# The MLP's u and gate products of two token pieces in seven products of halves for eight (Strassen's algorithm), with values and gated result kept in DRAM

## The chip, the cores and the metric

The kernel runs on one core of a Trainium2 chip. The core has five engines, each with its own queue that it works off in order: TensorE (PE: matrix products; PEld is its weight load), VectorE (DVE), ScalarE (ACT), GpSimd (POOL) and SyncE (SP), which here issues all DMAs. Products land in PSUM, a small memory that the other engines empty into SBUF; DRAM lies outside. The metric is device time in microseconds (us) of one execution. The kernel before has a median of 961.26 us in 3 runs (960.9 to 961.68).

## The reference

One inference step of two layers on 1024 prompt tokens and 64 sample tokens (8 sequences of 8), width 1024. The first layer is a gated linear attention, which the change leaves alone. The second is the one at stake:

```python
def cmlp_mixer(h, w_in, ln_g, ln_b, w_spatial, b_spatial, w_out):
    u, v, gate = jnp.split(h @ w_in, 3, axis=-1)
    v = layernorm(v, ln_g, ln_b)
    ...
    vg = v.reshape(bsz, n, c, CMLP_GROUPS, CMLP_GROUP_DIM)
    mixed = jnp.einsum('gts,bnsgd->bntgd', ws, vg) + bs.T[:, :, None]
    z = u * mixed.reshape(bsz, t, CMLP_WIDTH) * jax.nn.silu(gate)
    return z @ w_out, v
```

Before it, h = rmsnorm(x); behind it, x + z @ w_out goes through a last rmsnorm. The normalised v rows of the sample tokens are an output too.

## The kernel before, in words

The 1088 tokens are cut into three pieces (`PIECES`): piece 0 and piece 1 of 384 tokens (3 chunks of 128), and piece 2 of 256 prompt tokens and the 64 sample tokens. Activations lie transposed, features on the 128 partitions; width 1024 is `KT` = 8 slices of 128. To reach float32 accuracy, every operand of a large product is split into a high and a low part, and a product of slices takes three matmuls: high by high, high by low, low by high.

Weights come in blocks of 256 columns, each in four tiles of 128x512 (two slices by 256 columns). `fetch_w` (L89-97) loads such a tile from DRAM into one of three raw buffers (L93), makes the high part on ACT (L95) and the low part on DVE (L96), into a ring of eight `w` tiles. `fm_block` (L104-112) makes 128 columns of a block for one piece: 24 matmuls (L110) of 384 or 320 columns. `tm_block` and `tm_sample` (L114-142) do it with the tokens as rows. `split` (L167-174) makes the two parts of an activation.

In order of time:
- to about 478 us: the attention layer. To 541: its output product, `out_proj(12, ...)`, which leaves x in `x1_spill` in DRAM and the normed `h1` in SBUF, as parts.
- 541 to 640, the v stage: blocks 16 to 19, 9 groups each. ACT empties each group into the nine tiles of v (`vt`, `vs`) that stay in SBUF, L858; DVE gathers statistics, L864. Behind it the tiles are normalised in place, by ACT (L895) and DVE (L897) in turn.
- 640 to 848, the u/gate stage, L907-943: m = 0 to 7, one block (20 + m) each, with 128 columns of u and 128 of gate. For each piece: the gate product; DVE's scaling by the tokens' norm `rs` (L919); Silu on ACT (L920); a second scaling on POOL (L921); the mixing matmuls of v with `ws` (L924); gain and bias on DVE (L926); the u product; two DVE products (L935, L936) that leave z in SBUF. `fetch_w` gets the next block. `v_out` (L899-905) writes the sample rows of v. In m=7 z is split into `zs`.
- 848 to the end: `out_proj(28, ...)` on `zs`, and the last norm (L945-951).

A list scheduler in the build orders each engine's instructions from the program, by estimated times; so matmuls of different products stand interleaved, and the order on each engine is fixed before the launch. A tile with one buffer can be loaded again only when its last reader is done. SP too works in order: a DMA that waits holds all behind it.

Of the kernel before, what the change touches and what calls it, by code (L numbers as in the profile page):

```python
# [38 lines left out]
def trunk_kernel(ctx: ExitStack, tc: tile.TileContext, a: dict):  # L39
# [852 lines left out]
    for i, t in enumerate(tiles):  # L892
        r = t.shape[0]
        if i % 2:
            A.activation(t, t, AF.Identity, bias=lt[:r, i:i + 1], scale=lr[:r, i:i + 1])  # L895
        else:
            V.tensor_scalar(t, t, mv[:r, i, 0:1], lr[:r, i:i + 1], ALU.subtract, ALU.mult)  # L897

    def v_out(m):  # L899
# [3 lines left out]
        G.tensor_tensor(bc[:, 2, :], vs[:, cs], bc[:, 0, :], ALU.mult)  # L903
# [3 lines left out]
    z = [rp.tile([P, KT, n], F32, tag=f"raw{p}", name=f"z{p}") for p, n in enumerate(size)]  # L907
    zs = [None] * 3
    for m in range(KT):
        w = ws_[20 + m]  # L910
        g = m // 2
        fs = slice(m * P, (m + 1) * P)
        bias = mp.tile([P, P], F32, tag="bias", bufs=2, name="bias")
        V.scalar_tensor_tensor(bias, rsum[:, g, :], lnb[:, m:m + 1], bs[:, g, :], ALU.mult, ALU.add)
        for p, (t0, n, nch) in enumerate(PIECES):
            np_ = nch * P
# [2 lines left out]
            V.tensor_tensor(sg, ga, rs[p], ALU.mult)  # L919
            A.activation(sg, sg, AF.Silu)  # L920
            G.tensor_tensor(sg, sg, rs[p], ALU.mult)  # L921
# [149 lines left out]
```

## Time and profile before

| what | value |
|---|---|
| median of 3 runs | 961.26 us (960.9 to 961.68) |
| the profiled execution | 961.62 us, of which 959.8 us are the span that the profile shows |
| mean granted PE clock in it | 0.991 |
| DMA over the span | 77.62 MB, mean 81 GB/s |
| output product and norm, 848 to 960 us: PE busy | 100.58 of 112 us |

The page shows, under its second heading, the busy share of 40 equal slices in tenths. The u/gate stage is slices 27 to 35 (24 us each):

```profile
PE   8989999999999999989999999999999999999995
DVE  7888777677785787677543932254333333562246
ACT  8664545453553555363343622232111111353322
POOL 2023331323233232222241300004111011101123
```

A row of a group names line, engine and operation, what it writes and reads, its shape, its count, then busy time in us and mean ns of one, then the engine's idle time before them and what ended it. A chain row has start, length and what ran.

### The profile page before, as it was taken

What the parts mean: (1) busy time and instruction counts of PE and PEld (TensorE: products, weight loads), DVE (VectorE), ACT (ScalarE), POOL (GpSimd) and SP (SyncE); (2) the same over time, 40 slices, a digit from 0 to 9 for tenths busy, and PEclk for the clock granted to TensorE, in tenths of its full rate; (3) what the DMA queues carried; (4) which work ended last, traced back from release to release, by engine and by line L of the source; (5) the groups of instructions that cost most, each with busy time, mean ns of one, the idle gap of its engine ahead of it and who ended that gap; (6) DMA issues with size and microseconds to landing.
All of it is one profiled execution on the core that took longest, in us unless ns stands there. A gap on an engine that the chain in (4) does not pass through costs nothing.

```text
span 959.8 us, 16108 instructions
## 1 busy us (share of the span) xinstructions
PE 928.8 (97%) x6245; PEld 902.2 (94%) x6245; DVE 562.2 (59%) x1188; ACT 386.5 (40%) x800; POOL 210.4 (22%) x236
## 2 busy tenths in 40 slices
PE   8989999999999999989999999999999999999995
PEld 7979989999999899978999999999999999999994
DVE  7888777677785787677543932254333333562246
ACT  8664545453553555363343622232111111353322
POOL 2023331323233232222241300004111011101123
PEclk9999999999999999979999999999999999999998
DMA  9302113310231112423574321112101111123233
GB/s 294 91 1 81 51 34 88 106 44 29 78 114 36 61 62 72 130 90 105 159 248 153 93 70 45 45 45 83 31 26 44 44 45 44 45 59 92 60 112 128
DMA packets 71161, 77.62 MB, mean 81 GB/s; under 512 B 8470, under 2 KB 67676, under 8 KB 71084
## 3 DMA queue, kind: packets, MB, share of 16 engines
q1 hardware_dynamic: 71084, 76.58, 25.7%
q8 instruction: 49, 0.80, 0.3%
q14 instruction: 28, 0.23, 0.1%
HBM read 59.05 MB, written 17.51 MB: 80 GB/s over the span
## 4 chain that ended last, share of the span: by engine, by line
PE 73%; DVE 12%; ACT 5%; issue 4%; DMA 3%; POOL 1%; SPq 0%; DVEq 0%; ACTq 0%; POOLq 0%
PE fm L110 45%; PE tm L124 16%; PE sc L486 2%; PE mix L924 2%; DMA wr<-w 2%; PE o L591 1%; PE pst L552 1%; PE o L560 1%; PE tms L140 1%; PE o L562 1%; DVE scT L499 1%; DVE xl L451 1%; DVE w L96 1%; DVE xl L448 1%; ACT w L95 1%
## 5 line engine op out<-in xcount | busy, mean ns | idle before, releaser
L110 PE MATMUL fm<-h,w 128*128 128x384 f32 (+1 forms) x2208 | 388.9, 332 | 0.1
L110 PEld LDWEIGHTS fm<-h,w 128*128 128x128 f32 x2208 | 365.3, 188 | 2.2 <-DVE h L174 0.7
L124 PE MATMUL tm<-w,h 128*128 128x256 f32 (+1 forms) x1536 | 192.5, 282 | 0.3 <-DVE w L96 0.2
L124 PEld LDWEIGHTS tm<-w,h 128*128 128x128 f32 x1536 | 185.1, 188 | 1.6 <-DVE w L96 0.5
L96 DVE TENSOR_TENSOR w<-wr,w 128x512 fp32r<-128x512 f32 (+1 forms) x128 | 90.9, 726 | 34.5 <-ACT w L95 34.1
L110 PE MATMUL fm<-og,w 128*128 128x384 f32 (+1 forms) x576 | 104.1, 337 | 0.3 <-ACT og L170 0.3
L95 ACT ACTIVATE w<-wr 128x512 fp32r<-128x512 f32 (+1 forms) x128 | 78.3, 626 | 60.4 <-DMA wr<-w 36.6
L110 PEld LDWEIGHTS fm<-og,w 128*128 128x128 f32 x576 | 97.4, 192 | 2.1 <-DVE og L171 0.5
L110 PE MATMUL fm<-zs,w 128*128 128x384 f32 (+1 forms) x576 | 97.2, 330 | 0.4 <-DVE x L793 0.4
L110 PEld LDWEIGHTS fm<-zs,w 128*128 128x128 f32 x576 | 95.9, 188 | 1.3 <-DVE x L793 0.7
L920 ACT ACTIVATE sg<-sg 128x384 f32<-128x384 f32 (+1 forms) x24 | 12.2, 507 | 128.6 <-DVE sg L919 128.6
L793 DVE TENSOR_TENSOR x<-fm,res 128x384 f32<-128x384 f32 (+1 forms) x40 | 21.1, 528 | 69.5 <-PE fm L110 69.5
L921 POOL TENSOR_TENSOR sg<-sg,rs 128x384 f32<-128x384 f32 (+1 forms) x24 | 23.4, 975 | 165.8 <-ACT sg L920 165.8
L772 POOL TENSOR_TENSOR acc<-acc,sq 128x384 f32<-128x384 f32 (+1 forms) x30 | 31.3, 1045 | 110.4 <-ACT sq L767 109.8
L767 ACT ACTIVATE sq<-x 128x384 f32<-128x384 f32 (+1 forms) x42 | 20.9, 503 | 66.8 <-DVE x L793 65.3
L935 DVE TENSOR_TENSOR zt<-fm,zt 128x384 f32<-128x384 f32 (+1 forms) x24 | 12.8, 533 | 54.7 <-PE fm L110 54.7
L864 DVE BATCH_NORM_STATS2 st<-vt 128x6 f32<-128x256 f32 x32 | 13.6, 425 | 52.7 <-ACT vt L858 52.7
L441 POOL TENSOR_TENSOR xe<-xe,k 128x384 f32<-128x384 f32 (+2 forms) x24 | 29.1, 1214 | 45.4 <-ACT xe L440 45.3
L919 DVE TENSOR_TENSOR sg<-fm,rs 128x384 f32<-128x384 f32 (+1 forms) x24 | 12.8, 535 | 42.5 <-PE fm L110 42.5
L858 ACT ACTIVATE vt<-tm 128x256 f32<-128x256 f32 x32 | 12.3, 384 | 61.6 <-PE tm L124 61.6
L622 POOL TENSOR_TENSOR on<-on,g 128x384 f32<-128x384 f32 (+1 forms) x24 | 23.5, 1001 | 58.7 <-DVE on L621 35.9
L448 DVE TENSOR_TENSOR xl<-cum 128x192 f32<-128x192 f32 (+4 forms) x72 | 33.3, 492 | 0.0
(220 smaller groups left out, 1235.7 us busy)
## 6 DMA issues: line engine op xcount, KB each, us to landing
wr<-w SPq DMA_DIRECT2D x124, 256.0 KB, 3.3
s<-s SPq DMA_DIRECT2D x16, 256.0 KB, 5.6
state_s<-ns SPq DMA_DIRECT2D x32, 128.0 KB, 1.7
res<-x_spill SPq DMA_DIRECT2D x16, 192.0 KB, 2.4
y<-x SPq DMA_DIRECT2D x8, 384.0 KB, 2.4
x<-xt SPq DMA_DIRECT2D x7, 384.0 KB, 6.1
og_spill<-on SPq DMA_DIRECT2D x12, 192.0 KB, 1.9
ogr<-og_spill SPq DMA_DIRECT2D x12, 192.0 KB, 2.4
```

The source lines that it names most:

```text
L95: A.activation(w[:, 0], raw, AF.Copy)
L96: V.tensor_tensor(w[:, 1], raw, w[:, 0].bitcast(F32), ALU.subtract)
L110: PE.matmul(acc, lhs, rhs, start=(k == 0), stop=(k == 23))
L124: PE.matmul(acc, lhs, rhs, start=(k == 0), stop=(k == 23))
L441: G.tensor_tensor(xe, xe, kt_[:, :nl], ALU.mult)
L448: V.tensor_tensor(l3[:, :, lo:hi], c3[:, :, (i + 1) * m:], r, ALU.subtract)
L486: PE.matmul(bank[:, c, 0:192], xe[:, c * P:(c + 1) * P], xl[:, c * 192:(c + 1) * 192], start=True, stop=True)
L622: G.tensor_tensor(o, o, gate[h][:, j, t0:t0 + n], ALU.mult)
L767: A.activation(sq, raw[p][:, m, :], AF.Square)
L772: (V if gain is not None and p == 2 or m == KT - 1 else G).tensor_tensor(total, acc[p], sq, ALU.add)
L793: V.tensor_tensor(raw[p][:, m, :], pa, r, ALU.add)
L921: G.tensor_tensor(sg, sg, rs[p], ALU.mult)
```

## The change

For pieces 0 and 1 the block's product is one of 2 by 2 quarters. The rows of the result are u and gate, its columns piece 0 and piece 1; the summed index is cut into even and odd slices. So the weights have four quarters (quarter 1,1: u, even; 1,2: u, odd; 2,1: gate, even; 2,2: gate, odd) and `h1` has four (b11, b21: piece 0 even, odd; b12, b22: piece 1). Eight products of quarters become seven, with four sums of weight quarters (`s1` to `s4`) and four of token quarters (`tsum0` to `tsum3`). A product of quarters is 12 matmuls (`product`, L927). Piece 2 keeps its 48 matmuls of 320 columns.

What goes with it:
- The token sums are made once, in the v stage, one slice pair per block, from `x1_spill` (two DMAs of 384 KB, two ACT scalings, four POOL subtractions, four splits).
- The weight sums are made per block on POOL (L904: four of 128x512), each split on ACT (L891) and DVE (L892), and the plain quarters too: eight `w` tiles per block in place of four. The raw quarters of a block lie in one buffer, `rawq`, loaded by four DMAs of 256 KB (L886).
- v leaves SBUF: each group goes to DRAM (`v1_spill`, L943), and per m its 128 columns come back into one buffer `vm` (L985, L986) and are normalised by nine ACT instructions (L992).
- z goes to DRAM (`z_spill`, L1066 and L1097), and comes back for the split: piece 0 in m=7, pieces 1 and 2 behind the loop.
- The results of the seven products are combined by ACT copies (L1039, L1041, L1046), DVE adds out of PSUM (L1043, L1051, L1053) and POOL adds (L1047, L1048). Two PSUM banks (`two`: pb, pe) and one of the ring (`p1`) are added to by later products, behind the readers of the earlier ones.

```diff
-    vt = [mp.tile([P, D], F32, tag=f"vt{i}", name=f"vt{i}") for i in range(8)]
...
+    def raw_quarters(blk):
+        rw = mp.tile([P, 4, 2, 256], F32, tag="rawq", name="rawq")
+        for i in range(4):
+            SP.dma_start(rw[:, i], a["w256"][blk, i])
+        return rw
+
+    def parts_of(src):
+        w = wp.tile([P, 2, 4, P], F32R, tag="w", bufs=8, name="wq")
+        A.activation(w[:, 0], src, AF.Copy)
+        V.tensor_tensor(w[:, 1], src, w[:, 0].bitcast(F32), ALU.subtract)
+        return w
...
+        def sum(self, x, y, op):
+            t = wp.tile([P, 4, P], F32, tag="raw", bufs=3, name="qsum")
+            G.tensor_tensor(t, x, y, op)
+            return t
+
+        def sums(self):
+            q = self.q
+            s1 = self.sum(q[2, 1], q[2, 2], ALU.add)
+            s2 = self.sum(s1, q[1, 1], ALU.subtract)
+            self.w["s2"] = parts_of(s2)
+            self.w["s1"] = parts_of(s1)
+            self.w["s3"] = parts_of(self.sum(q[1, 1], q[2, 1], ALU.subtract))
+            self.w["s4"] = parts_of(self.sum(q[1, 2], s2, ALU.subtract))
...
+    def product(acc, w, b, start=True):
+        for k in range(4):
+            wh, wl, (bh, bl) = w[:, 0, k, :], w[:, 1, k, :], b[k]
+            for i, (lhs, rhs) in enumerate(((wh, bh), (wh, bl), (wl, bh))):
+                PE.matmul(acc, lhs, rhs, start=start and k + i == 0, stop=k + i == 5, skip_group_check=not start)
...
     for blk in range(16, 20):
...
+            SP.dma_start(v_d2[i * P:i * P + t.shape[0], cs], t)
...
+            if i == 6:
+                token_sums(blk - 16)
+            if (blk, i) == (18, 4):
+                nxt = Quarters(20)
+            if (blk, i) == (19, 1):
+                nxt.sums()
...
+    nxt.plain((1, 1), (1, 2), (2, 2), (2, 1))
...
+    def v_load(m):
+        t = up.tile([P, 9, P], F32, tag="vm", name="vm")
...
+        SP.dma_start(t[:, 0:8, :], v_d2[:SEQ, fs].rearrange("(c q) d -> q c d", q=P))
+        SP.dma_start(t[:NS, 8, :], v_d2[SEQ:, fs])
+        return t
...
     for m in range(KT):
...
+        for p in range(2):
+            mixed(zt[:, p, :], vm, g, m, bias, 3 * p, 3, False)
+        if m + 1 < KT:
+            nxt = Quarters(21 + m)
+        two = pp.tile([P, 2, 512], F32, tag="sc4", name="two")
+        pb, pe = two[:, 0, :N], two[:, 1, :N]
+        p6, p1 = tmp("sq", 2, N, "p6"), tmp("sq", 2, N, "p1")
+        product(pb, w["s2"], tq[1])
+        A.activation(p6, pb, AF.Copy)
+        product(pe, w["s3"], tq[2])
+        A.activation(sg[:, 1, :], pe, AF.Copy)
+        product(pb, w["s1"], tq[0], start=False)
+        V.tensor_tensor(sg[:, 1, :], sg[:, 1, :], pb, ALU.add)
+        pa = ps("mm", "p1")[:, :N]
+        product(pa, w[1, 1], b11)
+        A.activation(p1, pa, AF.Copy)
+        G.tensor_tensor(p6, p6, p1, ALU.add)
+        G.tensor_tensor(sg[:, 1, :], sg[:, 1, :], p1, ALU.add)
+        G.tensor_tensor(sg[:, 1, :], sg[:, 1, :], rs[1], ALU.mult)
+        product(pb, w["s4"], b22, start=False)
+        V.tensor_tensor(p1, p1, pb, ALU.add)
+        product(pe, w[2, 2], tq[3], start=False)
+        V.tensor_tensor(sg[:, 0, :], p6, pe, ALU.add)
...
+        product(pa, w[1, 2], b21, start=False)
+        mixed(z2, vm, g, m, bias, 6, 2, True)
...
+        if m + 1 < KT:
+            nxt.sums()
...
+            vm = v_load(m + 1)
+        u = ps("mm", "u")[:, :size[2]]
+        product(u, w[1, 1], quarter(2, 0))
+        product(u, w[1, 2], quarter(2, 1), start=False)
...
+            nxt.plain((1, 1), (1, 2))
...
+        ga = ps("mm", "gate")[:, :size[2]]
...
+        SP.dma_start(z_d[:, m, 2 * N:], z2)
+        if m + 1 < KT:
+            nxt.plain((2, 2), (2, 1))
+            v_norm(vm)
```

Three places show what the scheduler makes of it. A row is a line of the kernel, the operation, what it writes and reads (with buffer numbers), the shape and, behind an x, how often it stands there in a row.

DVE before, at the start of block 22 (m=2): `sg` is the gate, `zt` the mixed values, `w23_*` the parts of the next block's weights.

```order
L919 TENSOR_TENSOR sg_7464<-fm_7439,rs0_79 128x384
L926 SCALAR_TENSOR_TENSOR zt_7472<-mix_7468,lng_6103,bias_7437 128x384
L935 TENSOR_TENSOR zt_7472<-fm_7474,zt_7472 128x384
L936 TENSOR_TENSOR z0_7220<-zt_7472,sg_7464 128x384
L919 TENSOR_TENSOR sg_7536<-fm_7511,rs1_80 128x384
```

The next block's weight parts come only after the rows of the sample tokens, near the block's end, and nothing of PE's in this block waits for them. DVE in the changed kernel, from the end of the gate product of m=1 to the middle of m=2 (`wq_7846`, `wq_7849`: quarters 2,2 and 2,1 of m=2; `wq_7994`, `wq_7997`, `wq_8002`, `wq_8007`: s2, s1, s3, s4 of m=3; `z2`, `sg2`: piece 2 of m=1):

```order
L892 TENSOR_TENSOR wq_7846<-rawq_7637,wq_7846 128x512
L1093 TENSOR_TENSOR sg2_7840<-gate_7815,rs2_81 128x320
L892 TENSOR_TENSOR wq_7849<-rawq_7637,wq_7849 128x512
L1096 TENSOR_TENSOR z2_7626<-z2_7626,sg2_7840 128x320
L1008 SCALAR_TENSOR_TENSOR zt_7863<-mix_7866,lng_6101,bias_7861 128x384
L1008 SCALAR_TENSOR_TENSOR zt_7863<-mix_7871,lng_6101,bias_7861 128x384
L892 TENSOR_TENSOR wq_7994<-qsum_7992,wq_7994 128x512
L892 TENSOR_TENSOR wq_7997<-qsum_7990,wq_7997 128x512
L1043 TENSOR_TENSOR sg_7864<-sg_7864,two_7881 128x384
L892 TENSOR_TENSOR wq_8002<-qsum_8000,wq_8002 128x512
L1051 TENSOR_TENSOR p1_7883<-p1_7883,two_7881 128x384
```

Two low parts of weight sums stand ahead of L1043, which empties the bank that PE's s4 product adds to next. SP in the changed kernel at that place (`rawq_7876`: raw quarters for m=3):

```order
L985 DMA vm_7779<-v1_spill 128x8x128
L986 DMA vm_7779<-v1_spill 64x128
L886 DMA rawq_7876<-w256 128x512 x2
L1097 DMA z_spill<-z2_7626 128x320
L886 DMA rawq_7876<-w256 128x512 x2
L997 DMA bc_8013<-lnbc 64x256
L985 DMA vm_8018<-v1_spill 128x8x128
L1066 DMA z_spill<-zt_7863 128x384 x2
```

The spill of piece 2 of m=1 stands between the second and the third raw quarter; in m=3, 4 and 6 it stands between the first and the second. ACT in m=1, where the copy of p1 (L1046) stands behind three conversions of weight sums (s2, s1, s3 of m=2):

```order
L1039 ACTIVATE p6_7643<-two_7642 128x384
L1041 ACTIVATE sg_7625<-two_7642 128x384
L891 ACTIVATE wq_7755<-qsum_7753 128x512
L891 ACTIVATE wq_7758<-qsum_7751 128x512
L891 ACTIVATE wq_7763<-qsum_7761 128x512
L1046 ACTIVATE p1_7644<-p1_7684 128x384
L891 ACTIVATE wq_7768<-qsum_7766 128x512
```

So it is in m=1, 3, 4 and 6 of this stage; in m=2 and 5 the copy stands ahead of the four. On POOL the adds with p1 (L1047, L1048) stand behind three or four of the sums of the next block.

More of the change, by code (lines that the diff above doesn't have):

```diff
@@ L902, in v_out, with mixed @@
         SP.dma_start(bc[:, 0:2, :], a["lnbc"][m])
[L903 removed]
+        G.tensor_tensor(bc[:, 2, :], vm[:NS, 8, :], bc[:, 0, :], ALU.mult)
         G.tensor_tensor(bc[:, 2, :], bc[:, 2, :], bc[:, 1, :], ALU.add)
         SP.dma_start(a["v_out"][:, cs], bc[:, 2, :])
[L907 to L908 removed]
+    def mixed(dst, vm, g, m, bias, c0, nch, sample):
+        pm = ps("o", "mix")
+        for c in range(nch):
+            PE.matmul(pm[:, c * P:(c + 1) * P], vm[:, c0 + c, :], ws[:, g, :], start=True, stop=True)
+        n = nch * P
+        V.scalar_tensor_tensor(dst[:, :n].rearrange("p (c t) -> p c t", c=nch),
+                               pm[:, :n].rearrange("p (c t) -> p c t", c=nch), lng[:, m:m + 1],
+                               over(bias, nch), ALU.mult, ALU.add)
+        if sample:
+            PE.matmul(pm[:, n:n + NS], vm[:, 8, :], wss[:, g, :], start=True, stop=True)
+            V.scalar_tensor_tensor(dst[:, n:n + NS].rearrange("p (b t) -> p b t", b=NB),
+                                   pm[:, n:n + NS].rearrange("p (b t) -> p b t", b=NB), lng[:, m:m + 1],
+                                   over(bias[:, :8], NB), ALU.mult, ALU.add)
@@ new lines, in trunk_kernel @@
+        V.tensor_tensor(z2, u, z2, ALU.mult)
+        if m + 1 < KT:
+            nxt.plain((1, 1), (1, 2))
+        else:
+            zs[0] = act_slot(0, "zs0")
+            stage = mp.tile([P, 5, N], F32, tag="rawq", name="zstage")
+            SP.dma_start(stage, z_d[:, 0:5, 0:N])
+            more = [wp.tile([P, N], F32, tag="raw", bufs=3, name="zmore") for _ in range(2)]
+            for i, t in enumerate(more):
+                SP.dma_start(t, z_d[:, 5 + i, 0:N])
+            fetch_w(28, [0, 1])
+            split(zs[0], 7, zt[:, 0, :])
+            for kt in range(7):
+                split(zs[0], kt, stage[:, kt, :] if kt < 5 else more[kt - 5])
+            fetch_w(28, [2, 3])
@@ new lines, in trunk_kernel @@
+        ga = ps("mm", "gate")[:, :size[2]]
+        product(ga, w[2, 1], quarter(2, 0))
+        product(ga, w[2, 2], quarter(2, 1), start=False)
+        s2 = tmp("hn", 2, size[2], "sg2")
+        V.tensor_tensor(s2, ga, rs[2], ALU.mult)
+        A.activation(s2, s2, AF.Silu)
+        G.tensor_tensor(s2, s2, rs[2], ALU.mult)
+        V.tensor_tensor(z2, z2, s2, ALU.mult)
+        SP.dma_start(z_d[:, m, 2 * N:], z2)
+        if m + 1 < KT:
+            nxt.plain((2, 2), (2, 1))
+            v_norm(vm)
@@ L945, in x2_done @@
+    st6.close()
+    st4.close()
+    st7 = ExitStack()
+    zp = pool("zstage", stack=st7)
+    for p in (1, 2):
+        t0, n, _ = PIECES[p]
+        zs[p] = act_slot(p, f"zs{p}")
+        for i in range(2):
+            t = zp.tile([P, 4, N], F32, tag="z", bufs=3, name="z")[:, :, :n]
+            SP.dma_start(t, z_d[:, 4 * i:4 * i + 4, t0:t0 + n])
+            for kt in range(4):
+                split(zs[p], 4 * i + kt, t[:, kt, :])
     def x2_done(p, raw, rstd_tail):
```

146 lines of the change are left out of this document (85 added, 61 removed).

## The prediction

> **What bounds the kernel now.** I read the head of the page first, then the chain that ended last, then the stage that the change rewrites.
>
> ```profile
> span 959.8 us, 16108 instructions
> PE 928.8 (97%) x6245; PEld 902.2 (94%) x6245; DVE 562.2 (59%) x1188; ACT 386.5 (40%) x800; POOL 210.4 (22%) x236
> PE 73%; DVE 12%; ACT 5%; issue 4%; DMA 3%; POOL 1%; SPq 0%; DVEq 0%; ACTq 0%; POOLq 0%
> ```
>
> PE is busy for 97% of the span, and the chain lies on it for 73%. The windows view of the u/gate stage alone (the columns are in its first line):
>
> ```profile
> core 0: us, PE busy (x) PEld busy (x) DVE busy (x) ACT busy (x) POOL busy (x), PEclk, DMA share, GB/s
> 640.00:848.00 208.00, 207.29 (x1287) 205.77 (x1286) 89.05 (x173) 45.05 (x80) 29.66 (x39) 1.00 0.16 47
> ```
>
> Here PE is idle for 0.71 us in 208 at full clock, with the four others far from full. So a matmul removed here is time won, until another engine makes PE wait. The chain of waits gives the price of a matmul (start, us, what):
>
> ```profile
> 698.47 8.43 PE fm L110 x48
> 706.90 0.67 PE mix L924 x6
> 707.57 7.77 PE fm L110 x48
> ```
>
> Forty-eight matmuls of 384 columns take 8.43 us, 0.1757 each; 48 of which half have 320 columns take 7.77, so 24 x 0.1757 = 4.22 leaves 0.148 for each of those. A mix matmul is 0.67 / 6 = 0.11.
>
> **What is removed.** Per block m pieces 0 and 1 took 4 x 24 = 96 matmuls of 384 columns; seven products of 12 are 84. Twelve fewer, eight times: 12 x 8 x 0.1757 = 16.9 us off PE. The piece with the sample rows and the mixing keep their counts. Without any new wait the profiled execution of 961.62 us would become 944.7.
>
> **What is added beside PE.** The sums of weights are new on POOL, 4 per block of 128x512. The trace has one such shape, and two others as neighbours (columns: line, engine, operation, tile and shape, count, then busy us and mean ns, then idle before):
>
> ```profile
> L921 POOL TENSOR_TENSOR sg<-sg,rs 128x384 f32<-128x384 f32 x16 | 16.3, 1016 | 111.7 <-ACT sg L920 111.7
> L921 POOL TENSOR_TENSOR sg<-sg,rs 128x320 f32<-128x320 f32 x8 | 7.2, 894 | 54.0 <-ACT sg L920 54.0
> L845 POOL TENSOR_TENSOR ws<-ws,triu 128x512 f32<-128x512 f32 x1 | 1.7, 1727 | 0.0
> L441 POOL TENSOR_TENSOR xe<-xe,k 128x384 f32<-128x384 f32 x16 | 20.6, 1289 | 44.3 <-ACT xe L440 44.3
> ```
>
> From 320 to 384 columns L921 grows by 122 ns; two more such steps give 1.26 at 512, and I take 1.3. The ends are 1.02 (no dearer than 384 columns) and 1.73 (L845). The weight parts, the gate and the loads:
>
> ```profile
> L95 ACT ACTIVATE w<-wr 128x512 fp32r<-128x512 f32 x31 | 19.6, 632 | 25.9 <-DMA wr<-w 14.9 <-PE fm L110 8.0 <-DVE lm L883 1.6
> L96 DVE TENSOR_TENSOR w<-wr,w 128x512 fp32r<-128x512 f32 x32 | 22.1, 692 | 12.4 <-ACT w L95 12.4
> L919 DVE TENSOR_TENSOR sg<-fm,rs 128x320 f32<-128x320 f32 x8 | 3.9, 492 | 16.3 <-PE fm L110 16.3
> L920 ACT ACTIVATE sg<-sg 128x320 f32<-128x320 f32 x8 | 3.8, 470 | 55.0 <-DVE sg L919 55.0
> L919 DVE TENSOR_TENSOR sg<-fm,rs 128x384 f32<-128x384 f32 x16 | 8.9, 557 | 26.2 <-PE fm L110 26.2
> L920 ACT ACTIVATE sg<-sg 128x384 f32<-128x384 f32 x16 | 8.4, 526 | 73.6 <-DVE sg L919 73.6
> L581 ACT ACTIVATE kdm<-kds,rows 128x128 fp32r<-128x128 f32 x32 | 11.1, 395 | 6.9 <-PE psts L595 6.5 <-DVE kds L540 0.3
> ...
> L93 SPq DMA_DIRECT2D wr<-w x128: 328/546/662, 1.6 to 896.6; - x128
> ...
> DMA to landing us min/median/max: 2.6/3.3/6.2
> ...
> wr<-w SPq DMA_DIRECT2D x16, 256.0 KB, 4.0
> ...
> 482.00 5.80 DMA x<-x_spill
> ```
>
> The last four: a weight DMA occupies SP for 0.55 us (0.33 to 0.66) and lands 3.3 us after its issue (at least 2.6; 4.0 in the v stage). The 768 KB load at 482 us took 5.80. For vm (512 KB) I take 4.55, halfway between 3.3 and 5.80. One normalised chunk of vm on ACT: 0.33, between the 0.30 that L920's step of 56 ns for 64 columns leaves at 128, and L581's 0.395.
>
> **Where PE waits.** Before, weights went through three raw buffers long ahead. Now rawq has one buffer and is read up to the end of the block before. The wait comes from that. I walk block m=2 from G, the end of the gate product of m=1; the order rows shown with the change are those of this place.
> - ACT converts quarter (2,2), whose slot the gate product held: G+0.63; DVE's low part 1.32; L1093 (0.49) 1.81; Silu on ACT (0.47) 2.28; POOL's product (0.89) 3.2; DVE L1096 (0.49) 3.7.
> - SP stands at the spill of z2 until then, with rawq's third and fourth quarters behind it: z2 issues at 3.7, the quarters at 4.25 and 4.8, and the last lands at 8.1.
> - POOL's s1 needs all four: 9.4, and s2 10.7. ACT converts s2 by 11.33, s1 by 11.96; DVE's low part of s1 ends at 12.65.
> - These two low parts stand ahead of L1043 on DVE: it ends at 13.2. PE's s4 product adds into the bank that L1043 reads, and waits.
> - Unhindered, PE is there after 53 matmuls of 384 columns and 7 of the mixing: 53 x 0.1757 + 7 x 0.11 = 10.1. PE waits 3.1 us. The later wait, for L1051, is covered by s4 itself.
>
> The others go the same way, with other rows in between:
> - m=5 has the order of m=2: 3.1.
> - m=3 and m=6: three quarters instead of two stand behind z2 (0.55 more), and a second chunk of vm ahead of Silu; landing 8.7, L1043 at 13.8 against an unhindered 9.9: 3.9 each.
> - m=1: the copy of p1 (L1046) stands on ACT behind three conversions. Landing 8.5, third sum 12.4, conversion 13.0, copy (0.53) 13.6, POOL L1047 and L1048 (1.02 each) 15.6, DVE L1051 16.1. The seventh product (tsum3) waits for it; PE is there at 65 x 0.1757 + 7 x 0.11 = 12.2: 3.9.
> - m=4: the same with three quarters behind z2: landing 9.05, L1051 at 16.7: 4.5.
> - m=0: vm's load stands behind three quarters that wait for the conversion of the last one, done 2.3 after the v stage; it lands at 8.5, nine chunks and the copy of p1 end at 12.0, POOL's two at 14.0, L1051 14.6, against 12.5: 2.1.
> - m=7 has no sums: half a microsecond for vm.
>
> Together 2.1 + 3.9 + 3.1 + 3.9 + 4.5 + 3.1 + 3.9 + 0.5 = 25.0 us, in place of the 0.71 of before: 24.3 added.
>
> **What lies beside other work.** The v stage gets 36 spills (36 x 0.33 to 0.55 on SP, under 20 us of its 99), the token sums and block 20's parts. ACT, DVE and POOL have the room:
>
> ```profile
> 541.00:640.00 99.00, 99.00 (x843) 98.60 (x841) 38.25 (x81) 28.24 (x65) 6.79 (x7) 1.00 0.18 55
> ```
>
> Four rounds of two scalings, four conversions, four low parts and four subtractions are some 16 us for ACT, 9 for DVE, 16 for POOL. I cost it at nothing; if the first x1 loads catch the crowded DMA near 482 us (the 5.80 above), up to 1 us. The reload of z at the end has 8.5 us of PE's own work and then 4.2 us for each row block of piece 0 as cover; zs1 is ready about 1.5 us ahead of need: nothing, or up to 2 us if a landing takes the longest 6.2.
>
> **The sum.** -16.9 + 24.3 = +7.4 on the profiled execution's 961.62: **969.0 us**. The median of the runs shown, 961.26, is 0.36 lower, so I don't separate the two.
>
> Bounds: with landings at 2.6, issues at 0.33 and sums at 1.02, each of m=1 to m=6 loses about 1.8 us of its wait, m=0 about 1: 957. With sums at 1.73, POOL's 384 columns at 1.29, landings at 4.0 and vm's at 5.8, m=1, 3, 4 and 6 gain 2.5 each, m=2 and 5 1.6 to 2.5, m=0 1.3 to 2: 985.
>
> **Rivals.**
> - *The loads land early* (the other side). The mechanism is the landing of rawq's last quarter: each microsecond earlier takes one from each of six blocks. It decides at 7.4 / 6 = 1.2 us before my 8.1, at G+6.9. The least issue and landing give 3.7 + 0.33 + 0.33 + 2.6 = 6.96 in m=2, and cheap sums add to it. For it: 47 GB/s and a DMA share of 0.16 in this stage. Against: 3.3 is the median of that same quiet stage. It gives 957 to 963.
> - *Nothing waits*: the quarters would have to land at G+5.0, and z2's spill, ahead of two of them, is not ready before 3.7. For it only that the trace may hide slack I haven't seen: 944.7 to 950.
> - *POOL is slow under DVE*. The same 384 columns took 1016 ns in the quiet stage and 1289 (L441) where DVE was fuller; the new stage puts more on both. Sums near 1.7 and adds near 1.3 give 980 to 990.
>
> To this last one: the Trainium skill, "GPSIMD Engine Reference", section 1 (Specifications), says that POOL shares its SBUF interfaces with VectorE and contends with VectorE instructions that have two SBUF inputs. The two rows fit that rule, though they don't isolate it; by it the case of 980 to 990 would hold.
>
> **How the numbers follow.** Forecast (963.5 to 980) 0.52; early loads 0.25, of which 0.13 end below 959.3, 0.10 within 0.2% and 0.02 above; nothing waits 0.07; slow POOL 0.16. About 0.2% is what a measurement of this kernel can tell from no change. Faster 0.13 + 0.07 = 0.20, the same 0.10, slower 0.52 + 0.16 + 0.02 = 0.70. The range is 957 to 984: it leaves out "nothing waits", a little of the early loads and about half of slow POOL, some 0.18.
>
> **What would show it.** PE's count must fall by 96 in the u/gate stage, with its busy time about 16.9 us lower. Its idle time should be near 25 us, with one gap before s4 in m=2, 3, 5 and 6 (released by DVE L1043) and one before the seventh product in m=1 and 4 (released by L1051); rawq's last landing near G+8. POOL's 128x512 sums should read 1.3 us: 1.7 speaks for slow POOL. Landings near 2.6 and gaps of 1 to 2 us are early loads. If PE waits elsewhere (v stage, the reload of z, p1's bank), the walk is wrong, whatever the total says.

## The result, and the profile after

The changed kernel takes 992.87 us in the median of 4 runs (990.1 to 996.84), the kernel before 961.43 (960.9 to 961.68): a ratio of 1.0331, interval 1.0312 to 1.035. It is slower, as forecast, but by 31 us and not by 8, and outside the range of 957 to 984.

The line of the engines on the page of after, and the shares of the chain of waits:

```profile
PE 932.9 (94%) x6149; PEld 897.6 (90%) x6149; DVE 611.3 (61%) x1239; ACT 449.8 (45%) x940; POOL 306.0 (31%) x315
PE 57%; DVE 13%; DMA 9%; ACT 7%; POOL 6%; issue 6%; SPq 1%; DVEq 0%; ACTq 0%; POOLq 0%
```

PE has its 96 matmuls less (6149 for 6245), yet it is busy for longer: 932.9 us for 928.8. The chain lies on PE for 57%, before for 73%, and DMA's share went from 3 to 9%. So PE waits, and it also works more slowly: in some stretches its granted clock (PEclk below) is under 1.00.

The windows view, cut at the ends of stages and blocks (a block runs from the end of one gate product of the sample piece to the end of the next). First after: v stage, u/gate stage, then the eight blocks:

```profile
core 0: us, PE busy (x) PEld busy (x) DVE busy (x) ACT busy (x) POOL busy (x), PEclk, DMA share, GB/s
541.00:648.83 107.83, 101.39 (x835) 100.64 (x834) 49.42 (x96) 39.47 (x84) 24.44 (x22) 0.97 0.34 103
648.83:883.88 235.05, 210.20 (x1204) 201.07 (x1203) 119.24 (x195) 91.46 (x187) 103.69 (x99) 0.94 0.27 85
648.83:682.34 33.51, 28.88 (x155) 27.12 (x154) 17.95 (x36) 14.37 (x30) 12.90 (x13) 0.90 0.27 82
682.34:712.72 30.38, 27.46 (x151) 26.45 (x151) 14.42 (x23) 9.86 (x20) 14.25 (x13) 0.89 0.20 60
712.72:742.95 30.23, 26.22 (x151) 25.13 (x150) 16.53 (x23) 11.06 (x22) 14.00 (x13) 0.94 0.26 82
742.95:771.75 28.80, 24.81 (x153) 23.75 (x152) 14.28 (x23) 12.70 (x28) 13.26 (x13) 1.00 0.28 90
771.75:802.01 30.26, 27.51 (x151) 26.23 (x151) 14.11 (x24) 9.04 (x18) 13.92 (x13) 0.89 0.24 75
802.01:829.29 27.28, 24.74 (x151) 23.49 (x150) 15.87 (x23) 11.07 (x22) 14.47 (x13) 1.00 0.24 74
829.29:859.41 30.12, 26.12 (x153) 25.32 (x152) 13.04 (x22) 12.67 (x27) 13.09 (x13) 0.94 0.31 94
859.41:883.88 24.47, 24.47 (x151) 23.56 (x151) 13.04 (x23) 10.70 (x24) 7.79 (x8) 1.00 0.42 131
```

Before, the same cut of the u/gate stage (its v stage ended at 639.80):

```profile
639.80:848.00 208.20, 207.50 (x1287) 205.91 (x1286) 89.25 (x173) 45.23 (x81) 29.66 (x39) 1.00 0.16 47
```

The profiled executions differ by 996.84 - 961.62 = 35.2 us: 9.0 in the v stage, 26.9 in u/gate (235.05 for 208.20), and 0.7 less behind it. The last block, m=7, makes no sums and its PE is never idle: 24.47 us is about what a block takes unhindered. The seven others take 27.3 to 33.5. Of the four executions of after, the profiled one is the slowest; what follows from its trace adds up to 35.2 us, where the medians differ by 31.

PE's timeline at the holes of m=1 and m=2 (start, us, what, and in brackets the idle time before it and what ended it):

```profile
695.81 4.21 PE L927 MATMUL two<-h,wq 128*128 128x384 f32 x12 [2.92 <-DVE sg L1043]
715.74 0.49 PE L1006 MATMUL mix<-ws,vm 128*128 128x128 f32 x2 [1.79 <-ACT vm L992]
728.08 3.41 PE L927 MATMUL two<-h,wq 128*128 128x384 f32 x12 [2.22 <-DVE sg L1043]
```

The wait for L1043 in m=2 is the one forecast. The one for `vm` is not, and for m=1 the forecast named another wait, L1051. The 12 matmuls behind the first hole take 4.21 us where 12 x 0.1757 = 2.1 were expected: the granted clock is 0.50 from 694.97 to 701.80 us.

The chain of waits through m=2, from the gate product's end at 712.72 (G); the short rows between these are left out:

```profile
711.04 4.06 DMA vm<-v_spill
715.69 0.37 ACT sg L1094
716.20 0.89 POOL sg L1095
717.11 0.50 DVE z L1096
718.48 3.10 DMA rawq<-w
721.71 1.30 POOL qsum L904
723.07 1.30 POOL qsum L904
726.08 1.48 DVE wq L892
727.56 0.47 DVE sg L1043
```

From Silu on this is the walk of the prediction, step for step: Silu, POOL, z2, its spill, the late quarters, two sums, the low parts, L1043. Its first link, the late value piece, is not in the walk of m=2. It ends at G+15.3 (walk: 13.2).

### The profile page after: what moved, and what is told of

It reads as the page before. It is cut to its first block, busy times and chain, and to the rows that moved or that the text cites. A ratio compares the mean times of both kernels' runs of the same rounds, so it can differ in the third digit from the quotient of the medians.

```text
span 995.0 us, 16462 instructions
## 1 busy us (share of the span) xinstructions
PE 932.9 (94%) x6149; PEld 897.6 (90%) x6149; DVE 611.3 (61%) x1239; ACT 449.8 (45%) x940; POOL 306.0 (31%) x315
## 4 chain that ended last, share of the span: by engine, by line
PE 57%; DVE 13%; DMA 9%; ACT 7%; POOL 6%; issue 6%; SPq 1%; DVEq 0%; ACTq 0%; POOLq 0%
PE fm L110 25%; PE tm L124 13%; PE two L927 4%; DMA vm<-v_spill 3%; POOL qsum L904 2%; DMA rawq<-w 2%; PE u L927 2%; DMA xsum<-x_spill 2%; PE sc L486 2%; PE p L927 1%; PE o L591 1%; PE gate L927 1%; DMA wr<-w 1%; PE pst L552 1%; PE o L560 1%
## 5 line engine op out<-in xcount | busy, mean ns | idle before, releaser
L110 PE MATMUL fm<-h,w 128*128 128x384 f32 (+1 forms) x1056 | 188.8, 333 | 0.1
L110 PEld LDWEIGHTS fm<-h,w 128*128 128x128 f32 x1056 | 174.5, 188 | 1.7 <-DVE h L174 0.7
L96 DVE TENSOR_TENSOR w<-wr,w 128x512 fp32r<-128x512 f32 (+1 forms) x96 | 68.6, 732 | 29.4 <-ACT w L95 29.0
L927 PE MATMUL two<-tsum,wq 128*128 128x384 f32 x384 | 82.2, 356 | 2.9 <-DVE p L1051 2.9
L95 ACT ACTIVATE w<-wr 128x512 fp32r<-128x512 f32 (+1 forms) x96 | 58.3, 624 | 39.5 <-DMA wr<-w 21.9
L927 PEld LDWEIGHTS two<-tsum,wq 128*128 128x128 f32 x384 | 68.5, 193 | 7.5 <-DVE p L1051 4.2
L892 DVE TENSOR_TENSOR wq<-qsum,wq 128x512 fp32r<-128x512 f32 x32 | 32.3, 1035 | 41.7 <-ACT wq L891 41.4
L927 PE MATMUL p<-h,wq 128*128 128x384 f32 x192 | 45.0, 360 | 0.8 <-ACT p L1046 0.8
L942 DVE BATCH_NORM_STATS2 st<-vt 128x6 f32<-128x256 f32 (+1 forms) x36 | 15.0, 422 | 45.6 <-ACT vt L935 45.5
L891 ACT ACTIVATE wq<-qsum 128x512 fp32r<-128x512 f32 x32 | 19.1, 626 | 51.1 <-POOL qsum L904 29.0
```

The source lines that it names most:

```text
L95: A.activation(w[:, 0], raw, AF.Copy)
L96: V.tensor_tensor(w[:, 1], raw, w[:, 0].bitcast(F32), ALU.subtract)
L110: PE.matmul(acc, lhs, rhs, start=(k == 0), stop=(k == 23))
L892: V.tensor_tensor(w[:, 1], src, w[:, 0].bitcast(F32), ALU.subtract)
L927: PE.matmul(acc, lhs, rhs, start=start and k + i == 0, stop=k + i == 5, skip_group_check=not start)
```

## The experiments

The orders of before, after and e6 are the list scheduler's. In the other kernels the order on each engine is written out in a table; except in e5 it is the changed kernel's with only the moves shown or named. "Block" is a block as cut above. All medians and intervals:

| run | us, median | ratio to before | v stage ends | u/gate stage, us |
|---|---|---|---|---|
| before | 961.43 | 1 | 639.8 | 208.2 |
| after | 992.87 | 1.0331 (1.0312 to 1.035) | 648.8 | 235.1 |
| e1_busy | 989.19 | 1.0304 (1.0275 to 1.0333) | 646.4 | 229.9 |
| e2_zlate | 987.59 | 1.0281 (1.0257 to 1.0304) | 649.5 | 227.3 |
| e3_vstage | 987.22 | 1.0272 (1.0254 to 1.0289) | 642.2 | 234.5 |
| e4_raw2 | 970.31 | 1.01 (1.0085 to 1.0115) | 647.1 | 209.7 |
| e5_full | 1015.08 | 1.0563 (1.0537 to 1.059) | 644.9 | 254.8 |
| e6_eight | 971.23 | 1.0107 (1.0091 to 1.0123) | 640.6 | 215.1 |
| e7_vm2 | 992.91 | 1.0335 (1.0314 to 1.0356) | 649.1 | 230.6 |
| e8_nosums | 973.55 | 1.0132 (1.0112 to 1.0151) | 647.8 | 213.6 |
| e9_best | 966.47 | 1.0048 (1.0034 to 1.0062) | 640.4 | 213.9 |
| e10_half | 973.98 | 1.0128 (1.0112 to 1.0144) | 640.5 | 220.1 |
| e11_without | 959.55 | 0.9985 (0.9976 to 0.9994) | 642.4 | 205.7 |
| e12_best2 | 960.42 | 0.9992 (0.9982 to 1.0002) | 641.2 | 206.6 |

### e1: is it the half clock?

```diff
+        for k, n in _BUSY.get(m, ()):
+            scratch = ps("misc", "busy")
+            extra[k] = [PE.matmul(scratch[:, :N], tsum[0][:, 0, 0, :P], tsum[0][:, 0, 0, :], start=True, stop=True).ins
+                        for _ in range(n)]
```

Matmuls whose product nobody reads stand in PE's queue at the holes of m=0 to 6, at each as many as fit into it, 125 in all.

> The changed kernel with every instruction held to its order on its engine, and idle matmuls (128x384, into a PSUM bank that nobody reads) put into PE's queue right ahead of 13 matmuls that waited in the u/gate stage, as many as fit into the wait seen there. Nothing else differs; the output is the reference's. Theory 'clock': in the changed kernel's u/gate stage PE ran 27 us at half the granted clock, in stretches of 3.4 or 6.8 us right behind its waits, and half of that is lost. Filled waits keep the clock: granted clock 0.98 or more in that stage (0.94 without), time down by 9 to 14 us from 992.9, to 979-984. Rival 'waits alone': the lower clock only goes with the idling and costs nothing; then the time stays within 3 us of 992.9, or rises by what the idle matmuls delay.

The u/gate stage of e1 in the windows view:

```profile
646.44:876.33 229.89, 220.98 (x1329) 211.15 (x1328) 118.87 (x195) 91.63 (x187) 104.36 (x99) 1.00 0.28 87
```

The clock is full throughout (1.00 for 0.94), and the stage is only 5.2 us shorter, the kernel 3.7, between the theory (9 to 14) and its rival (at most 3). The two medians are of four runs each and their intervals overlap, so the size of this gain is uncertain. But after had 27 us at half clock in this stage; had all of it counted, filling the holes would have won some 13. At full clock PE comes sooner to the same instruction and waits there longer, so the half clock falls mostly into time in which PE would wait anyway. The waits themselves, with eight blocks at 24.4 unhindered, are 229.9 - 195.2 = 34.7 us. That is an upper estimate: the idle that is left (8.9 us) and 125 x 0.1757 of idle matmuls make 30.9.

### e2 and e4: the late quarters

e2, SP in m=2 (the other blocks alike):

```diff
 DMA rawq<-w256 128x512 x2
-DMA z_spill<-z2 128x320
 DMA rawq<-w256 128x512 x2
+DMA z_spill<-z2 128x320
```

> The changed kernel in its own order, but on SP the spill of z2 goes behind the fourth raw quarter instead of ahead of two or three of them (m=1 to 6). Theory 'z2 holds the quarters': the last quarter issues 1.0 to 1.7 us earlier per block, six times, and some half-clock stretches shrink with the waits: 7 to 12 us less, 981-986. Rival 'the quarters wait for rawq itself' (the release by the last low part, which stands behind the vm chunks on ACT): less than 3 us.

e4, a second buffer, with the four loads of each block queued a block earlier:

```diff
-        rw = mp.tile([P, 4, 2, 256], F32, tag="rawq", name="rawq")
+        into, tag = (mp, "rawq") if blk % 2 == 0 else (up, "rawr")
+        rw = into.tile([P, 4, 2, 256], F32, tag=tag, name=tag)
```

> The changed kernel in its own order, but odd blocks use a second buffer of raw quarters, and on SP each block's four loads go a block earlier. Theory: the waits for L1043 and L1051 in m=1 to 6 (16 us in the trace) come from the late quarters; they go, and the half-clock stretches behind them (some 20 us, 10 us lost) with them: 20 to 27 us less, 966-973. What stays are m=0 and the waits for vm. Rival: the chain through vm (load, chunk, Silu of piece 2, POOL) or POOL's own order takes the quarters' place: 5 to 12 us less.

e2 gave 5.3 us, less than the theory's 7 to 12 and more than the rival's 3; e4 gave 22.6, as expected. The stage lost 25.4 us (209.7 for 235.1), with every sum, addition and spill still in it. In the windows view m=2 (703.86 to 730.02) went from 30.23 to 26.16; what it still waits for is `vm`. The late quarters are the main cause, and z2's spill in front of them is a part of it.

### e3: the v stage

e3, ACT at the third of four token sums (`vt` is the copy that frees a bank for PE); the second and fourth are moved back likewise, and their loads on SP for the third and fourth:

```diff
 ACTIVATE hn<-tms 64x256
-ACTIVATE xsum<-xsum,vecs 128x2x384 x2
-ACTIVATE tsum<-xsum 128x384
 ACTIVATE w_3<-wr_3 128x2x256
-ACTIVATE vt<-tm 128x256
-ACTIVATE tsum<-xsum 128x384 x3
...
+ACTIVATE vt<-tm 128x256 x5
+ACTIVATE xsum<-xsum,vecs 128x2x384 x2
+ACTIVATE vt<-tm 128x256
+ACTIVATE tsum<-xsum 128x384 x4
```

> The changed kernel in its own order, but in the v stage the scalings and splits of the token sums 1, 2 and 3 (ACT, DVE) stand 3 to 9 groups later, and the loads of x1 for sums 2 and 3 behind later spills. Theory: PE's 6.4 us of waiting in the v stage come from ACT standing at the x1 load with evacuations behind it, and 6.8 us at half clock follow; both go: 8 to 10 us less, 983-985, v stage back at about 99 us. Rival: the spills and loads of the stage are too many for SP or the DMA queues, and PE waits there just as much in other places: less than 3 us.

After's chain (the loads for the second and the third sum) and ACT's timeline at the third, rows between left out, then the row of PE:

```profile
554.05 4.04 DMA xsum<-x_spill
566.26 6.99 DMA xsum<-x_spill
```

```profile
573.32 1.76 ACT L871 ACTIVATE xsum<-xsum,vecs 128x768 f32<-128x768 f32 x2 [5.61 <-DMA xsum<-x_spill]
576.43 0.38 ACT L935 ACTIVATE vt<-tm 128x256 f32<-128x256 f32 x1
```

```profile
576.87 13.94 PE L124 MATMUL tm<-w,h 128*128 128x256 f32 x96 [4.25 <-ACT vt L935]
```

ACT stands 5.61 us at a scaling whose load isn't there, with the `vt` copy queued behind it, and PE waits 4.25 us for that copy. Moved back, the stage ends 6.6 us sooner and the kernel gains 5.65, less than the 8 to 10 expected; a later load left one wait of 2.5 us. A stage with PE busy for 99.00 of 99.00 us and slack on ACT had no slack in ACT's order.

### e6 and e8: what Strassen costs, and what the spills

e6 keeps spills, loads and quarters, but makes the eight plain products, without sums of either kind:

```diff
-        product(pb, w["s2"], tq[1])
-        A.activation(p6, pb, AF.Copy)
...
+            product(ga, w[2, 1], quarter(p, 0))
+            product(ga, w[2, 2], quarter(p, 1), start=False)
```

> The change without Strassen: v and z still go through DRAM, rawq and vm have one buffer, but pieces 0 and 1 take the eight plain products of quarters (96 matmuls) and there are no token sums and no weight sums. Theory: the spills alone cost little, a microsecond or so of waiting for vm per block at most; the loss hangs on the sums, which put the late quarters on PE's path: 960-968, and no half clock behind gaps. Rival: the spilling itself (SP, DMA, reloads) costs the time: 975 or more.

```profile
640.55:855.63 215.08, 211.73 (x1299) 207.34 (x1299) 81.19 (x155) 65.43 (x141) 31.52 (x47) 1.00 0.29 92
```

This is e6's u/gate stage in the windows view. The kernel is some 10 us slower than before, with no Strassen in it; the theory's top was 968. In the profiled executions 6.9 of it are in u/gate, of which 3.35 is idle (its longest hole, 1.77 us in m=0, ends with a chunk of `vm`) and the rest longer busy time of PE (211.73 for 207.50), 0.75 in the v stage, and 1.9 behind. The 36 spills of v themselves cost the v stage next to nothing; the token sums did. From e6 to after, 21.6 us are Strassen's own, where the removed matmuls alone should have given -16.9; as e6 was ordered anew, some of this may be the order's.

e8 makes the parts of s1 to s4 from plain quarters, without the sums on POOL; products and additions stay:

```diff
-            s1 = self.sum(q[2, 1], q[2, 2], ALU.add)
-            s2 = self.sum(s1, q[1, 1], ALU.subtract)
-            self.w["s2"] = parts_of(s2)
+            self.w["s2"] = parts_of(q[2, 2])
...
```

> The changed kernel in its own order without the weight sums on POOL: the parts s1 to s4 are made from plain quarters, so the products are of wrong operands; everything else runs. Theory: two to four sums of 1.3 us each stand between the last quarter and PE's wait in m=1 to 6, and slow DVE's low parts from 0.70 to 1.08 us beside them: 3 to 4 us per block, 18 to 25 us less, 968-975. Rival: without the sums PE waits for the release of rawq or for vm just as long: 8 us less or fewer.

```profile
647.80:861.40 213.60, 203.05 (x1204) 194.64 (x1203) 114.74 (x196) 91.70 (x187) 68.67 (x71) 0.98 0.31 94
```

The stage takes 213.6 us, 21.5 less, and the kernel 19.3 less. The quarters are as late as before (in m=2 the last is issued at G+6.3, in after at G+5.8), yet PE no longer waits for L1043. So without sums the same late quarters do little harm: it is quarters and sums in one chain, late load, then 2.6 us of sums, then parts, that holds PE. Without the sums POOL is also less busy beside DVE's low parts, which shortens them (see the rivals below); the run doesn't separate the two.

### e5 and e7: the value pieces

e5 has e4's and e3's edits in an order made anew, and `vm` split into a tile of six chunks and one of three (`vn`). In its queue on SP the load of the six stands behind z2's spill and the quarters:

```diff
-        t = up.tile([P, 9, P], F32, tag="vm", name="vm")
...
+        t = up.tile([P, 6, P], F32, tag="vm", name="vm")
+        SP.dma_start(t, v_d2[:6 * P, fs].rearrange("(c q) d -> q c d", q=P))
+        t2 = up.tile([P, 3, P], F32, tag="vn", name="vn")
```

> The changed kernel with what the first four runs pointed to, together: two buffers of raw quarters loaded a block earlier, vm cut into chunks 0 to 5 and the rest so that its load can start once pieces 0 and 1 are mixed, vm's first load ahead of the quarters on SP, the token sums of the v stage later. If the lost time is these waits and nothing else, the u/gate stage comes near 8 x 24 = 192 us and the v stage near 99, and the whole to 945-952, faster than the kernel before. Rival: POOL and DVE slow each other in the fuller order and a new wait (L1043, L1051, Silu) takes over: 955-965.

It took 1015.08 us, 63 above the top of the theory and 50 above the rival's. ACT in e5's timeline:

```profile
725.53 1.26 ACT L1040 ACTIVATE vm<-vm,lt,lr 128x128 f32<-128x128 f32 x3 [7.79 <-DMA vm<-v_spill]
```

ACT stood 7.79 us at the chunks of `vm`, and the copy behind them (`sg`, L1089), which empties the bank PE needs next, came that late: PE stood 6.87 us for it. The fault is my order's, so the run says nothing on the split.

e7 gives `vm` a second buffer and loads it a block earlier, in the changed kernel's order:

```diff
-        t = up.tile([P, 9, P], F32, tag="vm", name="vm")
+        t = up.tile([P, 9, P], F32, tag="vm", bufs=2, name="vm")
```

> The changed kernel in its own order, but vm has two buffers and its loads for m=2 to 7 stand on SP a block earlier. Theory: the prediction's walk went wrong in good part by vm, which landed 2.4 us behind the gate product instead of 1.3 and held Silu of piece 2, z2's spill and the quarters; with vm ahead of time the blocks m=1 to 6 lose 1 to 2 us each, 6 to 12 us with the clock: 981-987. Rival: the conversions of rawq and POOL set the time, vm lies beside them: less than 3 us.

No change: 992.91 for 992.87. PE's waits for `vm` are gone behind m=0, and the one at L1089 (which is L1043 in after's numbering) grew, in m=2:

```profile
724.49 3.56 PE L973 MATMUL two<-h,wq 128*128 128x384 f32 x12 [3.59 <-DVE sg L1089]
```

2.22 became 3.59. The quarters were the later of two waits in a row, so curing the earlier one moved it.

### e9 to e12: putting the cures together

> The changed kernel's order with four edits together: a second buffer for the raw quarters, each block's first half loaded a block earlier; the token sums later in the v stage; in the first u/gate block the first value piece loaded ahead of the quarters and the copy of the first p1 behind the chunk scaling; in each later block the next value piece loaded ahead of the z spill, with the two GpSimd operations of the value output behind the second p1 sum. Theory (the time is lost in three places, which add: the late quarters about 22 us, the token sums 5.7, what the spills leave of waits at the value chunks 5 to 10): 953 to 958 us, below the kernel before; the u/gate blocks at 24.5 to 25.5 each, sum 198 to 202 us; the v stage ends at 642. Rival (a wait moved is a wait made elsewhere, as in the run that split the value loads): 962 to 970, with new gaps ahead of the quarters' or the next block's products. Below 950 would mean that the spills cost nothing where they stand now.

> The same without the last of the four edits: the value pieces of the later blocks are loaded behind the z spill, as in the changed kernel, and the GpSimd operations of the value output stay. Theory: 970.3 of the second raw buffer alone, less the 5.7 that the token sums gave alone, less 3 to 6 of the first block, whose 30.9 us should come to 25 to 28: 958 to 962 us; the waits at the value chunks of 0.8 to 1.5 us in blocks 1 to 6 stay, some 6 us in all, and are the difference from the run with all four. Rival: the difference from the run with all four is within 1 us, because the value pieces aren't late, as two value buffers in the unmended kernel gave nothing.

> The run of four edits again, without its edit of the first u/gate block (that block keeps the changed kernel's order): the second raw buffer, the later token sums, and from block 1 on the value piece loaded ahead of the z spill. In the run of four edits blocks 2 to 7 took 24.3 to 26.2 us, but block 0 took 30.0 and block 1 35.4. Theory (the edit of block 0 made this: VectorE's lo parts put later held GpSimd's fourth sum, Silu and so the release of the value buffer): block 0 at 29 to 31 and block 1 at 25 to 26.5, the u/gate stage at 203 to 207 us, 956 to 960 us in all. Rival (the buffers' own fault: the second half's quarters and the value pieces contend on the queue in block 1): block 1 stays over 30, and the time at 963 to 968.

> The run of four edits again, with another edit of the first u/gate block: the first value piece is loaded ahead of the quarters and the copy of the first p1 stands behind the sixth chunk, as there, but VectorE's lo parts stay in the changed kernel's order (only the first of them behind the add to p1), and GpSimd makes its two operations on p6 and the gate sum ahead of the second weight sum. Theory: block 0 at 25 to 28 us and block 1 at 25 to 26, the u/gate stage at 198 to 204 us, 952 to 957 us in all, below the kernel before by 0.4 to 1 per cent. Rival (what is won in block 0 is lost in block 1, whose loads wait for block 0's reads): 957 to 963.

The edit of the later blocks, on SP in m=3 (e4 against e11); with it the small `bc` load and, in m=1, 2, 4 and 5, POOL's two operations that read the value piece go ahead, so that the one buffer `vm` comes free in time:

```diff
+DMA vm<-v_spill 128x8x128
+DMA vm<-v_spill 64x128
 DMA z_spill<-zt 128x384 x2
 DMA v_out<-bc 64x128
-DMA vm<-v_spill 128x8x128
-DMA vm<-v_spill 64x128
```

and those of block 0 in e9, on SP (`rawr`: the quarters for m=1) and on DVE (`qsum`: parts of the sums for m=1), with e4's line numbers. The three low parts come back behind the mixing of the sample rows, and ACT's copy of p1 goes behind the sixth chunk. e12 has the moves on SP and ACT; on DVE only the first low part moves, behind L1098, and POOL's two adds go ahead of the second sum (second fence):

```diff
+DMA vm<-v_spill (both parts)
 DMA rawr<-w256 128x512 x3
-DMA vm<-v_spill (both parts)
 DMA rawr<-w256 128x512
...
-L939 TENSOR_TENSOR wq<-qsum,wq 128x512
 L1098 TENSOR_TENSOR p<-p,two 128x384
-L939 TENSOR_TENSOR wq<-qsum,wq 128x512 x2
 ...
 L1100 TENSOR_TENSOR sg<-p,two 128x384
```

```diff
 L951 TENSOR_TENSOR qsum<-rawr 128x512
+L1094 TENSOR_TENSOR p<-p,p 128x384
+L1095 TENSOR_TENSOR sg<-sg,p 128x384
 L951 TENSOR_TENSOR qsum<-qsum,rawr 128x512
 L951 TENSOR_TENSOR qsum<-rawr 128x512
-L1094 TENSOR_TENSOR p<-p,p 128x384
-L1095 TENSOR_TENSOR sg<-sg,p 128x384
```

e9 and e10, which share the edits of block 0, missed by 8 and 12 us; e9's rival held. In e9 blocks 2 to 7 took 24.3 to 24.6, as expected, but for 26.3 in m=4; m=1 took 35.37. Rows of e9's timeline, POOL in m=0, then PE in m=1:

```profile
665.79 1.68 POOL L952 TENSOR_TENSOR qsum<-rawr,qsum 128x512 f32<-128x512 f32 x1 [6.60 <-DVE wq L940]
```

```profile
678.11 1.65 PE L1057 MATMUL mix<-ws,vm 128*128 128x128 f32 x6 [7.64 <-ACT vm L1040]
```

POOL's fourth sum waits 6.60 us for a buffer that a low part still reads, since I had put the low parts later. Silu, POOL's next steps and the release of `vm` all follow, and PE waits 7.64 us. e11, without that edit, has m=1 at 25.99, its theory's figure. Its block m=2 in the windows view:

```profile
699.93:724.47 24.54, 24.54 (x152) 23.61 (x151) 15.61 (x23) 11.73 (x24) 13.03 (x13) 1.00 0.28 93
```

m=2 has no idle time left, though every sum and addition is made. In e10, where the value pieces load behind the z spill and POOL's two operations stay where they were, m=2 is 28.54 and m=3 25.81; in e9, 24.53 and 24.33. Once the quarters come in time, the value pieces are the next wait: e10's rival falls. e12 kept m=1 whole (25.75), but m=0 went to 32.55, so its hope of 952 to 957 missed; the 960.42 lies where its rival put it, by another mechanism, since the loss was in block 0 itself; why was not followed up.

e11 is the best version: 959.55 us, faster than the changed kernel by 3.4% and than before by 0.15% (0.06 to 0.24), which is about the limit of what can be told; e12's interval overlaps it. e11 isn't free of waits either: its block 0 takes 31.51 us, some 6 to 7 more than the others, and its v stage 2.6 more than before.

## Why the prediction was wrong

**The mechanism in u/gate was right in the main, but not all of it.** Late raw quarters, then sums, then low parts ahead of L1043 and L1051: e4 and e8 each broke the chain at one link and took most of the stage's loss away, and in m=2 to 6 there are holes before the products named. But of the 24.85 us of idle PE only 15.6 end with L1043 or L1051. At chunks of `vm` PE idled 6.3 us, in m=0, 2, 3, 5 and 6, where the walk had no hole; in m=0 2.1 us more ahead of the mixing of the sample rows; and in m=1 it stopped a product early, at L1043. By the prediction's own sign ("If PE waits elsewhere ... the walk is wrong") these places and the v stage count against it. The sums took 1.3 us as taken (L904 in the groups below), POOL's adds not.

```profile
L904 POOL TENSOR_TENSOR qsum<-rawq 128x512 f32<-128x512 f32 x14 | 18.0, 1284 | 44.3 <-DMA rawq<-w 44.3
L892 DVE TENSOR_TENSOR wq<-qsum,wq 128x512 fp32r<-128x512 f32 x28 | 29.8, 1084 | 40.3 <-ACT wq L891 39.9
L1047 POOL TENSOR_TENSOR p<-p,p 128x384 f32<-128x384 f32 x8 | 10.7, 1337 | 10.2 <-ACT p L1046 10.2
L992 ACT ACTIVATE vm<-vm,lt,lr 128x128 f32<-128x128 f32 x64 | 26.4, 481 | 10.3 <-DMA vm<-v_spill 10.3
```

These are after's groups of the u/gate stage. Against the profiled 996.84 us the forecast of 969.0 is 27.8 short. By its own steps (the sizes are differences of single executions):

- **"I cost it at nothing; ... up to 1 us"** (v stage): 9.0 us. This is the step that failed outright. It counted ACT's work and not its order: a load that is awaited at the head of ACT's queue holds the copies that free PE's banks. e3 shows 5.7 to 6.6 of the 9.0 to be that; the rest was not taken apart.
- **"Together ... 25.0 us"** of waits: at most 34.7, from e1. By e1's blocks less 24.4, m=0 was mis-sized most (6.9 for 2.1), then m=3 and m=6 (5.9 and 5.8 for 3.9 each). In m=2 the real chain is 2.1 us behind the walk, in two places. The value piece lands at G+2.4 and holds Silu, so DVE L1096 ends at G+4.9 and not 3.7; one chunk on ACT took 0.481 where 0.33 was taken. And the low parts of sums took 1.08 us each where 0.69 was taken from the quiet stage; that DVE might slow down beside POOL was no term of the walk. POOL's 384 columns took 1.34 for 1.02.
- **"12 x 8 x 0.1757 = 16.9 us off PE"**: some 12.3 came. Before, a block's PE was busy 207.50 / 8 = 25.94 us; unhindered it is now 24.4, 1.54 less and not 2.11. (By PE's busy time in e11, 197.57 us at full clock, only 9.9 came, and the waits in e1 were 32.3; the sum of the two steps is the same.) The pace shows why. From e11 and from e6, where each next row's start ends the one above:

```profile
707.89 2.38 PE L975 MATMUL two<-tsum,wq 128*128 128x384 f32 x12
710.11 1.03 PE L975 MATMUL p<-h,wq 128*128 128x384 f32 x5
```

```profile
839.39 4.32 PE L926 MATMUL ga<-h,wq 128*128 128x384 f32 x24
843.55 4.32 PE L926 MATMUL up<-h,wq 128*128 128x384 f32 x24
```

  That is 2.22 / 12 = 0.185 us each against 4.16 / 24 = 0.173. Start by start, e6's stand 0.173 or 0.174 apart; in e11's twelve the first takes 0.276 and the others 0.174 to 0.180. Such single long steps, about 0.09 us each, stand mostly where PE goes from one product to another. The u/gate stage of before has 33, 2.8 us in all; after's, interleaved from shorter products, has some 80, about 7 us. That is most of the 4.6 missing. What causes a long step was not tried.
- **The half clock** stands nowhere in the prediction: 5.2 us in u/gate by e1, uncertain as said there.

The sum: 9.0 + 9.7 + 4.6 + 5.2 = 28.5 too little, and 0.7 too much for what lies behind; 27.8. That the terms close says nothing by itself, since the split between waits, pace and clock follows from the choice of 24.4 and from e1's total.

One number agreed by chance. "Its idle time should be near 25 us": PE was idle for 235.05 - 210.20 = 24.85. But some 10 us of the waiting passed as matmuls at half clock, and count as busy. Idle time confirms a sum of waits only where the clock is full.

**The rivals.** Early loads and no waits are out: the last quarter landed at G+8.9. Slow POOL under DVE was half right: its sums stayed at 1.3, not 1.7, its adds were near 1.3, and it was DVE's low parts that stretched most, 1.08 us from `qsum` against 0.70 from `rawq`. By "GPSIMD Engine Reference", section 1 (Specifications), in the Trainium skill, POOL and two-input VectorE instructions contend. The trace of e8 agrees, and there the tile can't be the cause, since all 60 low parts read `rawq`. The 30 during which POOL was idle took 0.67 to 0.69 us; the 12 with POOL at work from start to end took 1.09 in the mean and up to 1.53. One of each, from m=1:

```profile
688.96 0.69 DVE L938 TENSOR_TENSOR wq<-rawq,wq 128x512 fp32r<-128x512 f32 x1 [4.60 <-ACT wq L937]
694.85 1.12 DVE L938 TENSOR_TENSOR wq<-rawq,wq 128x512 fp32r<-128x512 f32 x1
```

So the rival had the contention right, but priced it on POOL alone; in m=2 the stretch that lay in the chain ahead of L1043 was DVE's. How much of the 27.8 us it is, no run shows.

## What to carry to other kernels

A change that removes matmuls from a full PE pays only if each helper's queue still has its loads in time: walk every in-order queue past the new instructions, in the stage where they are added as well as in the one where they are used. If two waits stand in a row, curing the earlier one alone shows nothing (e7), and its worth appears only after the later one is gone (e10 against e9). And ask first what can remain when the waits are cured: here the spills alone cost some 10 us (e6) of the 16.9 counted, and the best order tried, with 6 to 7 us of waits left in its first block, ends 0.15% ahead.

## What the runs showed of the hardware

**The clock halves after short holes.** Twelve matmuls took 4.21 us behind a hole of 1.97 in m=4, and 2.35 behind one of 2.18 in m=5 (rows between left out):

```profile
785.09 1.14 PE L927 MATMUL p<-h,wq 128*128 128x384 f32 x5 [0.77 <-ACT p L1046]
788.20 4.21 PE L927 MATMUL two<-tsum,wq 128*128 128x384 f32 x12 [1.97 <-DVE p L1051]
815.89 2.35 PE L927 MATMUL two<-h,wq 128*128 128x384 f32 x12 [2.18 <-DVE sg L1043]
```

So the length of one hole didn't decide it. The clock records show what did. Within a profile, from 541 us on, the stretches at half clock are 3.41 or 6.83 us long and start on one grid of 3.41 us. The windows view of after on that grid:

```profile
783.71:787.12 3.41, 1.75 (x9) 1.10 (x7) 2.04 (x3) 1.23 (x3) 2.29 (x3) 1.00 0.00 0
787.12:793.95 6.83, 5.75 (x18) 5.75 (x19) 2.49 (x4) 0.89 (x2) 4.05 (x4) 0.50 0.00 0
814.43:817.84 3.41, 1.95 (x11) 1.95 (x12) 2.91 (x3) 0.00 (x0) 2.72 (x3) 1.00 0.00 0
```

In m=4 the hole of 0.77 and a part of the next fell into one window, 1.66 us of idle PE in 3.41, and the half clock followed. In m=5 the window's edge cut the hole of 2.18 into 0.7 and 1.46, and none followed. In the fourteen profiles, from 541 to 865 us, each of the 41 full-clock windows ahead of a half-clock stretch held 1.66 us of idle PE or more, and of the other 1230 only five held as much (1.66 to 1.81). So here the clock halved when PE was idle for about half of a window, and where the holes fell on the grid decided. The grid lies differently in each profile, which may be why after's four executions, with granted clocks of 0.984, 0.982, 0.979 and 0.976, take 990.1, 991.98, 993.76 and 996.84 us; that was not shown, as one of the four has a trace. The Trainium skill, "TensorE: Matmul & The Clock Gate", section "HAM oscillation — how this bites in real kernels", gives as its abstract rule that PE should have no idle gap over about 3.4 us. Here shorter holes already led to half clock. That cost little where PE went on to wait anyway (e1): 5.2 us of the stage, 3.7 of the median.

**The same load differs by its moment.** The 384 KB of `xsum` took 4.04 us when issued at 554 us and 6.99 at 566 (rows with e3), `vm`'s 512 KB 4.06 us in m=2 and 6.89 when issued at 652.53, behind three quarters.
